# A fp32 decoder layer on one core: DeltaNet's last two units put beside the merge's loads, the MLP's sums put on VectorE, and the RMSNorm ahead of the MLP applied behind its square

## Chip, core and metric

One core of a Trainium2 chip runs the kernel. The metric is the device time of an execution in microseconds. Engines are called by the profile's names: PE is TensorE, DVE is VectorE, ACT is ScalarE, POOL is GpSimd, SP is the engine whose queue issues all DMAs here.

## What is computed

One layer of a decoder with d = 1024, 1024 positions and a hidden width of 4096, all in fp32. Cut to what the change touches:

```python
mix = sigmoid(g_dn) * (o_dn @ W_dn) + sigmoid(g_ns) * (o_ns @ W_nsa)
x   = x + mix @ W_out
h2  = x * rsqrt(mean(x * x, axis=-1) + EPS) * gain
x   = x + square(relu(h2 @ W_up)) @ W_down
```

Ahead of it stand the first RMSNorm, the input projections, a gated DeltaNet (o_dn) and a sparse attention with three branches (o_ns).

## The kernel before

**Number format.** Activations lie with features on the 128 partitions and with positions in the free dimension, in two halves of 512. A fp32 product is made of three matmuls on parts of 32 bits of a shorter mantissa: each operand is split into a high part, copied by ACT (L174), and a low part, which DVE makes by subtracting the high part from the operand (L186, and L277 for weights that `unit` loads); then PE sums high·high, high·low and low·high (`gemm`, L188). So every 128x512 block of weights or activations costs one ACT and one DVE instruction before PE can use it.

**Stages that the change touches**, in order of time in the profile. The sparse attention runs to about 1578 us; its pieces, and the 16 DeltaNet units (half, c) of `dn_part` and `dn_gate` between them, are queued with due times by `at3` and emitted in the order of these times. A DeltaNet unit is 24 matmuls of 128x512 into one bank `g` of the pool `ga`; then `dn_gate` loads the gate's input `gtd` into `th` (one buffer), makes (th + 1) * y on DVE (L1352) and stores the result in the scratch tensor `mxd`. The last two units, c = 6 and 7 of half 1, are due behind everything else. Then comes the merge (`ns_rows`, `ns_merge`; 16 units of 24 matmuls): `ns_rows` loads eight rows of `ond`, the attention's output, through four buffers and splits them; `ns_merge` multiplies them by `w_pn`, gates the result, adds `mxd` (on POOL) and splits the sum. `out_proj` (16 units of 24 matmuls, about 1677 to 1768 us) multiplies by `w_o`, adds x, stores it as `x1d` and sums its squares. `root` turns the sums into 1/sqrt(mean + EPS), with small matmuls, a power on POOL, and a matmul that spreads the result over the partitions; `norm_first` (half 0) and `norm_second` (half 1) multiply x by it and make the sums that the up stage needs.

**MLP.** Both products use Winograd's form of Strassen's scheme, with seven products instead of eight. Up: for each of 16 n, seven products p of 12 matmuls (`up_mm`), whose weights are blocks a11, a12, a21, a22 or sums of them (`weights_of`) and whose other operands are B11, B21, B22 and the sums T1 to T4 (`SIDE`), all made once. `up_out` applies relu and the square on ACT; `up_sums` makes the sums that the down stage wants; all go to the scratch tensor `acd`. Down: for each of two n, seven products of 8 times 12 matmuls (`down_mm`), whose order is in `turns`; the sums of weights and the low parts are made five products ahead (`down_prep`, LEAD). Weights come by `down_load`, activations `bb` from `acd` by `down_side`, x by `x_load`.

**What sets the order.** The program is written as one stream; a scheduler reorders it for each engine by data, buffers and priorities, and each engine then runs its list in that order. SP too: a DMA in its list waits until its data and its buffer are ready, and all later DMAs wait behind it. A pool of buffers that is opened in the place of another waits for all readers of the old one.

Of the kernel before, what the change touches and what calls it, by code (L numbers as in the profile page):

```python
# [20 lines left out]
D = 1024  # L21
# [125 lines left out]
def body(ctx: ExitStack, tc: tile.TileContext, A, out):  # L147
# [74 lines left out]
    for half in range(2):  # L222
# [3 lines left out]
        if half == 0:  # L226
            load_consts(cp, 0)
            cp_raw = [wp.tile([128, 4, 128], F32, name="wr", bufs=3) for _ in range(2)]
            for i in range(2):
                SY.dma_start(cp_raw[i], A["w_cp"][0][:, 4 * i:4 * i + 4])  # L230
# [49 lines left out]
    def unit(src):  # L280
        ks = []
        for i in range(2):
            wr = wp.tile([128, 4, 128], F32, name="wr", bufs=3)
            SY.dma_start(wr, src[:, 4 * i:4 * i + 4])
            ks += parts(wr)
# [181 lines left out]
    def cmp_hidden(u, i):  # L467
# [3 lines left out]
        w1 = wp.tile([128, 4, 128], F32, name="wr", bufs=3)  # L471
# [444 lines left out]
    def fill_nb(u):  # L916
# [3 lines left out]
        def prep():  # L920
            for kp in range(4):
                wr = wp.tile([128, 2, 256], F32, name="wr", bufs=3)
# [415 lines left out]
    def dn_part(half, c, j):  # L1338
        oh, ol = D_["o", half]
        ks = D_["w", half, c]  # L1340
        if j == 0:
            D_["y"] = PL.ga.tile([128, 512], F32, name="g")
# [5 lines left out]
    def dn_gate(half, c):  # L1348
        sl = slice(half * 512, half * 512 + 512)
        th = PL.pr.tile([128, 512], F32, name="th", bufs=1)  # L1350
        SY.dma_start(th, gtd[c, :, sl])
# [4 lines left out]
    for half in range(2):  # L1356
        at3(0.2 + 16 * half, dn_rows, half)
        for c in range(8):
            e = 1.5 + 2 * (8 * half + c)
            if half and c >= 6:  # L1360
                e = 22 + 2 * c
# [15 lines left out]
    shut("po", "pm", "pT", "pS", "ga", "pr")  # L1377
    pool("pf", 4, side="right")
    bank("pq", 4)
# [8 lines left out]
    for half in range(2):  # L1388
        rows_o.append([PL.py.tile([128, 8, 512], F32R, name="o") for _ in range(2)])
        mixes.append([big(True) for _ in range(2)])  # L1390
# [7 lines left out]
    def ns_merge(c, half):  # L1398
# [10 lines left out]
        GP.tensor_tensor(md, md, th, OP.add)  # L1409
        act(mh[:, c], md, AF.Copy, scale=0.5)  # L1410
        V.scalar_tensor_tensor(ml[:, c], md, 0.5, f(mh[:, c]), op0=OP.mult, op1=OP.subtract)

    ns_rows(0)
    for c, half in [(0, 0), (1, 0), (0, 1), (1, 1)] + [(c, half) for c in range(2, 8) for half in range(2)]:
# [7 lines left out]
    x1, sums = [[], []], [None, None]  # L1422
# [3 lines left out]
    def out_proj(half, c):  # L1426
# [9 lines left out]
        SY.dma_start(x1d[c, :, HALF[half]], x)  # L1436
        if c == 0:
            sums[half] = t512(PL.p5, "u", 4)
            act(sums[half], x, AF.Square)
        else:  # L1440
            sq = t512(PL.pw, "tmp", 2)
            act(sq, x, AF.Square)
            (V if half else GP).tensor_tensor(sums[half], sums[half], sq, OP.add)

    def root(half):
        return root_rows(sums[half], PL.pq, "Q", PL.pw, PL.p5.tile([128, 4], F32, name="r4", bufs=1), 2)
# [3 lines left out]
    def sub(o, a, b, eng=None):  # L1450
        (eng or GP).tensor_tensor(o, a, b, OP.subtract)
# [3 lines left out]
    def parts_of(n, src, i, eng=V):  # L1455
        act(R[n][:, i], src)
        sub(R[n][:, 4 + i], src, f(R[n][:, i]), eng)

    def norm_first(r):
        R["raw"] = raw = f(big(False))  # L1460
        R["B11"], R["B21"] = big(True), big(True)
        for k in range(8):
            V.scalar_tensor_tensor(raw[:, k], x1[0][k], cols[:, 8 + k:9 + k], r, op0=OP.mult, op1=OP.mult)
            parts_of("B21" if k >= 4 else "B11", raw[:, k], k % 4)

    def norm_second(r):
        raw = R["raw"]
        R["T2"], R["T3"] = big(True), big(True)
        b12, b22, t = [], [], []

        def head(j):
            b12.append(t512(PL.p5, "b", 4))
            V.scalar_tensor_tensor(b12[j], x1[1][j], cols[:, 8 + j:9 + j], r, op0=OP.mult, op1=OP.mult)
            sub(raw[:, j], b12[j], raw[:, j], V)
            b22.append(t512(PL.p5, "c", 8))
            V.scalar_tensor_tensor(b22[j], x1[1][4 + j], cols[:, 12 + j:13 + j], r, op0=OP.mult, op1=OP.mult)

        def second(j):
            t.append(t512(PL.p5, "c", 8))
            sub(t[j], b22[j], raw[:, j], V)  # L1480
            parts_of("T2", t[j], j)

        head(0)
        for j in range(4):
            if j < 3:
                head(j + 1)
            second(j)
        yield
        for j in range(4):
            sub(b12[j], b22[j], b12[j])  # L1490
            parts_of("T3", b12[j], j)
# [259 lines left out]
```

## Time and profile before

| what | us |
|---|---|
| time, median of 3 executions (lowest, highest) | 2409.52 (2408.16, 2412.6) |
| the profiled execution's own time | 2409.07 |
| its span in the trace | 2407.3 |
| PE busy in the span | 2339.8 |
| DVE busy | 1563.8 |
| ACT busy | 1093.4 |
| POOL busy | 569.0 |

In the timelines a row is: start and duration in us, engine, line of the kernel, operation, output tile <- input tiles, size, number of instructions that are drawn together; in brackets stands how long the engine was idle before it, and which instruction or DMA ended that. SPq rows are DMAs being issued. [...] A matmul's own duration overlaps the next one's, so its pace is read from the starts.

### The profile page before, as it was taken

What the parts mean: (1) busy time and instruction counts of PE and PEld (TensorE: products, weight loads), DVE (VectorE), ACT (ScalarE), POOL (GpSimd) and SP (SyncE); (2) the same over time, 40 slices, a digit from 0 to 9 for tenths busy, and PEclk for the clock granted to TensorE, in tenths of its full rate; (3) what the DMA queues carried; (4) which work ended last, traced back from release to release, by engine and by line L of the source; (5) the groups of instructions that cost most, each with busy time, mean ns of one, the idle gap of its engine ahead of it and who ended that gap; (6) DMA issues with size and microseconds to landing.
All of it is one profiled execution on the core that took longest, in us unless ns stands there. A gap on an engine that the chain in (4) does not pass through costs nothing. (4 is left out here: it accounts for less than half of the span.)

```text
span 2407.3 us, 44378 instructions
## 1 busy us (share of the span) xinstructions
PE 2339.8 (97%) x16673; PEld 1916.8 (80%) x16673; DVE 1563.8 (65%) x3626; ACT 1093.4 (45%) x2258; POOL 569.0 (24%) x473
## 2 busy tenths in 40 slices
PE   7999999999999999999999999999999999989999
PEld 5887878787878887877777777778878888878887
DVE  6766664747484838348877777643397666596785
ACT  4233343434344444227666766532355555534443
POOL 3132321203231423000010111012145444260320
PEclk9999999999999999999999999999999999999999
DMA  5421313131212221237432422164425443566333
GB/s 176 135 65 56 85 43 94 42 91 44 80 50 82 51 77 50 87 116 179 131 115 72 115 89 73 32 225 161 148 83 172 144 149 136 204 232 225 109 126 102
DMA packets 237510, 267.37 MB, mean 111 GB/s; under 512 B 76976, under 2 KB 128496, under 8 KB 237168
## 3 DMA queue, kind: packets, MB, share of 16 engines
q1 hardware_dynamic: 237296, 264.55, 35.2%
q8 instruction: 131, 2.15, 0.4%
q14 instruction: 83, 0.68, 0.1%
HBM read 190.05 MB, written 72.38 MB: 109 GB/s over the span
## 5 line engine op out<-in xcount | busy, mean ns | idle before, releaser
L177 PE MATMUL g<-hh,wh 128*128 128x512 f32 (+1 forms) x816 | 335.4, 411 | 8.2 <-ACT hh L174 7.3
L177 PE MATMUL g<-hl,wh 128*128 128x512 f32 (+1 forms) x816 | 327.4, 401 | 0.1
L177 PE MATMUL g<-hh,wl 128*128 128x512 f32 (+1 forms) x816 | 323.5, 396 | 0.0
L177 PE MATMUL V<-big,wh 128*128 128x512 f32 x768 | 239.4, 392 | 1.6 <-DVE c L1594 1.6
L186 DVE TENSOR_TENSOR wl<-a,wh 128x512 fp32r<-128x512 f32 x192 | 160.6, 838 | 111.0 <-ACT wh L174 110.9
L174 ACT ACTIVATE wh<-wr 128x512 fp32r<-128x512 f32 x210 | 132.1, 630 | 207.1 <-PE g L177 131.4
L174 ACT ACTIVATE wh<-a 128x512 fp32r<-128x512 f32 x192 | 121.1, 631 | 219.6 <-PE V L177 109.5
L1223 DVE CUSTOM_DVE_ANT_0 junk<-S,cst 128x384 f32<-128x384 f32 (+3 forms) x320 | 168.4, 533 | 56.8 <-PE S L177 52.7
L277 DVE TENSOR_TENSOR wl<-wr,wh 128x512 fp32r<-128x512 f32 x178 | 123.6, 698 | 111.9 <-ACT wh L174 108.4
L177 PEld LDWEIGHTS g<-hh,wh 128*128 128x128 f32 (+1 forms) x816 | 153.6, 188 | 36.2 <-ACT hh L174 7.5
L174 ACT ACTIVATE P<-T 128x512 f32<-128x512 f32 x228 | 134.0, 597 | 100.9 <-PE T L177 88.9
L177 PEld LDWEIGHTS g<-hh,wl 128*128 128x128 f32 (+1 forms) x816 | 153.4, 188 | 29.5 <-issue 0.6
L177 PEld LDWEIGHTS g<-hl,wh 128*128 128x128 f32 (+1 forms) x816 | 153.8, 188 | 26.4 <-DVE hl L324 0.8
L177 PEld LDWEIGHTS V<-big,wh 128*128 128x128 f32 x768 | 144.7, 189 | 32.7 <-ACT c L174 1.2
L177 PE MATMUL V<-big,wl 128*128 128x512 f32 x384 | 150.5, 392 | 3.2 <-DVE wl L186 3.2
L177 PE MATMUL g<-wh,hh 128*128 128x256 f32 x512 | 147.4, 288 | 0.0
L177 PE MATMUL g<-wl,hh 128*128 128x256 f32 x512 | 144.8, 283 | 0.0
L177 PE MATMUL g<-wh,hl 128*128 128x256 f32 x512 | 144.8, 283 | 0.0
L1272 POOL TENSOR_TENSOR acc<-acc,bs 128x256 f32<-128x256 f32 x62 | 48.9, 789 | 401.3 <-DVE bs L1270 286.9
L177 PEld LDWEIGHTS o<-vv,P 128*64 128x64 f32 x3648 | 116.0, 138 | 27.1 <-issue 20.4
L177 PE MATMUL o<-vv,P 128*64 128x65 f32 x3648 | 130.1, 225 | 0.0
L177 PE MATMUL S<-ks,qc 96*128 96x384 f32 (+3 forms) x320 | 127.1, 409 | 1.6 <-DVE mx L1223 1.4
(371 smaller groups left out, 5709.1 us busy)
## 6 DMA issues: line engine op xcount, KB each, us to landing
bb<-acd SPq DMA_DIRECT2D x112, 256.0 KB, 2.8
wr<-in_w_dn_dram SPq DMA_DIRECT2D x64, 256.0 KB, 2.9
a<-in_w_u_dram SPq DMA_DIRECT2D x64, 256.0 KB, 3.4
acd<-c SPq DMA_DIRECT2D x64, 256.0 KB, 3.0
a<-in_w_d_dram SPq DMA_DIRECT2D x64, 256.0 KB, 4.9
wr<-in_w_nb_dram SPq DMA_DIRECT2D x32, 256.0 KB, 2.7
wr<-in_w_gt_dram SPq DMA_DIRECT2D x32, 256.0 KB, 2.7
gtd<-fx SPq DMA_DIRECT2D x32, 256.0 KB, 2.2
```

What stands on the lines that cost most here:

```text
L174: return SC.activation(o, i, fn, **kw)
L177: return PE.matmul(o, l, r, start=start, stop=stop, skip_group_check=True)
L186: V.tensor_tensor(lo, src, f(hi), OP.subtract)
L277: V.tensor_tensor(wl, wr, f(wh), OP.subtract)
L1223: V.tensor_tensor_reduce(junk[:, :w], ps[:, :w], mask[:, a:b], 1.0, 3e38, OP.add, OP.min, o)
L1272: adds.tensor_tensor(acc, acc, b, OP.add)
```

## The change

1. The DeltaNet units c = 6 and 7 of half 1 leave the schedule of the sparse stage. Only their weights are loaded there. They are written behind the first `ns_rows`; their gates' inputs are loaded into two buffers of the merge's pool; c = 7 sums in a bank of its own (pool `pT`); the pools of the sparse stage are closed behind them.
2. Raw weights of `unit` are staged in the pool `cq` (3 buffers), which is closed before the merge; from then on in two buffers `a22` of the merge's pool `pw`. Before, three buffers in a pool that stays open served all stages.
3. All sums of tiles in SBUF run on DVE; POOL had them: the merge's 16 sums, 7 sums of squares, and most sums of the MLP.
4. Since relu(r·z)² = r²·relu(z)², the MLP starts from x times gain, which ACT makes in `out_proj`; r² = 1/(mean + EPS) comes from one matmul with a matrix of ones, a multiply and add, and a DVE reciprocal of 128x512 for each half; `up_out` multiplies by it (four products for each n). The sums for half 1 are made within `out_proj`.
5. Down, n = 0: product order 4, 2, 1, 5, 6, 3, 7 instead of 1, 2, 6, 5, 7, 3, 4; the blocks a22 are loaded first, a11 later; x tiles are loaded in another order.

```diff
-            cp_raw = [wp.tile([128, 4, 128], F32, name="wr", bufs=3) for _ in range(2)]
+            cp_raw = [PL.cq.tile([128, 4, 128], F32, name="wr", bufs=3) for _ in range(2)]
...
     def unit(src):
...
-            wr = wp.tile([128, 4, 128], F32, name="wr", bufs=3)
+            if hasattr(PL, "pw"):
+                wr = PL.pw.tile([128, 512], F32, name="a22", bufs=2).rearrange("p (a b) -> p a b", a=4)
+            else:
+                wr = PL.cq.tile([128, 4, 128], F32, name="wr", bufs=3)
...
-            D_["y"] = PL.ga.tile([128, 512], F32, name="g")
+            D_["y"] = PL.pT.tile([128, 512], F32, name="T") if half and c == 7 else PL.ga.tile([128, 512], F32, name="g")
...
             if half and c >= 6:
-                e = 22 + 2 * c
+                at3(e - 0.5, dn_weights, half, c)
+                continue
...
-        GP.tensor_tensor(md, md, th, OP.add)
+        V.tensor_tensor(md, md, th, OP.add)
...
+    ths = []
+    for c in (6, 7):
+        ths.append(t512(PL.pw, "a12"))
+        SY.dma_start(ths[-1], gtd[c, :, HALF[1]])
     ns_rows(0)
+    for c in (6, 7):
+        for j in range(4):
+            dn_part(1, c, j)
+        dn_gate(1, c, ths[c - 6])
+    shut("po", "pm", "pT", "pS", "ga", "pr")
+    pool("pf", 4, side="right")
+    bank("pq", 4)
...
         SY.dma_start(x1d[c, :, HALF[half]], x)
+        if half == 0:
+            y = raw[:, c]
+        else:
+            y = t512(PL.p5, *(("b", 4) if c < 4 else ("c", 8)))
+            (b12 if c < 4 else b22).append(y)
+        act(y, x, AF.Copy, scale=cols[:, 8 + c:9 + c])
...
-            (V if half else GP).tensor_tensor(sums[half], sums[half], sq, OP.add)
+            V.tensor_tensor(sums[half], sums[half], sq, OP.add)
...
     def root(half):
-        return root_rows(sums[half], PL.pq, "Q", PL.pw, PL.p5.tile([128, 4], F32, name="r4", bufs=1), 2)
+        p = t512(PL.pq, "Q")
+        mm(p, K("ones"), sums[half], True, True)
+        rr[half] = r = sums[half]
+        V.tensor_scalar(r, p, 1.0 / D, EPS, op0=OP.mult, op1=OP.add)
+        V.reciprocal(r, r)
...
-    def sub(o, a, b, eng=None):
-        (eng or GP).tensor_tensor(o, a, b, OP.subtract)
+    def sub(o, a, b):
+        V.tensor_tensor(o, a, b, OP.subtract)
...
+    def norm_second(j):
+        sub(raw[:, j], b12[j], raw[:, j])
+        t2s.append(t512(PL.p5, "u", 4))
+        sub(t2s[j], b22[j], raw[:, j])
+        sub(b12[j], b22[j], b12[j])
+        sub(raw[:, 4 + j], raw[:, 4 + j], t2s[j])
...
-            GP.tensor_tensor(a21, a21, a22, OP.add)
+            V.tensor_tensor(a21, a21, a22, OP.add)
...
         act(x, x, AF.Square)
+        r = rr[p in (0, 3)]
+        V.tensor_tensor(x, x, r, OP.mult)
...
-    turns = [(1, 2, 6, 5, 7, 3, 4), (2, 1, 5, 6, 3, 7, 4)]
+    turns = [(4, 2, 1, 5, 6, 3, 7), (2, 1, 5, 6, 3, 7, 4)]
...
-            DW[n, i, b] = t = t512(PL.pg if d == 0 else PL.ph, b, J)
+            DW[n, i, b] = t = t512(PL.pg if m else PL.ph, b, J)
...
-        if n and p == 1:
+        if p == 1:
             sub(w["a11"], w["a11"], w["a21"])
-        e = q - J - 5
-        if 0 <= e < J:
-            sub(DW[0, e, "a11"], DW[0, e, "a11"], DW[0, e, "a21"])
...
         if (half, c) == (1, CB):
-            norm_first(root(0))
+            root(0)
+            norm_first()
+        if half and c >= 4:
+            norm_second(c - 4)
+    norm_parts("T2")
...
-        if q == 2:
-            second = norm_second(root(1))
-        if q in (2, 7, 8):
-            next(second)
+        if q in (2, 4, 6, 8):
+            norm_parts(("T3", "T4", "T1", "B22")[q // 2 - 1])
+        if q == 3:
+            root(1)
```

How the change stands in the engines' lists, at three places. **SP where the merge begins**, before (a_18952 to a_18980 are the first eight rows of `ond`, a_18996 and a_18997 the inputs of the first merge unit's gate):

```order
L1404 DMA a_18996<-gtd 128x512
L1353 DMA mxd<-th 128x512
L1395 DMA a_18968<-ond 128x512
L1395 DMA a_18972<-ond 128x512
L1395 DMA a_18976<-ond 128x512
L1351 DMA th<-gtd 128x512
L1395 DMA a_18980<-ond 128x512
L1405 DMA a_18997<-mxd 128x512
L1395 DMA a_19029<-ond 128x512
L1395 DMA a_19033<-ond 128x512
L1353 DMA mxd<-th 128x512
```

and with the change (a_18878 and a_18880 are the two gates' inputs and then their results, a_18882 to a_18910 the eight rows, a_18984 and a_18990 the raw weights of the first merge unit):

```order
L1396 DMA a_18894<-ond 128x512
L1357 DMA mxd<-a_18878 128x512
L1396 DMA a_18898<-ond 128x512
L1396 DMA a_18902<-ond 128x512
L1396 DMA a_18906<-ond 128x512
L1396 DMA a_18910<-ond 128x512
L1357 DMA mxd<-a_18880 128x512
L287 DMA a_18984<-in_w_pn_dram 128x512
L287 DMA a_18990<-in_w_pn_dram 128x512
L1405 DMA a_18996<-gtd 128x512
L1406 DMA a_18997<-mxd 128x512
```

The loads of the two gates' inputs now stand ahead of the rows, and the loads of `w_pn`, which stood among the last items of the sparse stage, stand behind the store of the last gate.

**DVE at the first root**, before (tile r is 128x4; wl<-wr are low parts of `w_o`):

```order
L1435 TENSOR_TENSOR c<-c,V 128x512
L241 TENSOR_SCALAR r_20137<-Q 128x4
L277 TENSOR_TENSOR wl<-wr,wh 128x512
L1443 TENSOR_TENSOR u<-u,tmp 128x512
L252 TENSOR_TENSOR tmp<-cst_114,r_20137 128x512
L277 TENSOR_TENSOR wl<-wr,wh 128x512
L1463 SCALAR_TENSOR_TENSOR big<-a_19659,cols,Q 128x512
L1463 SCALAR_TENSOR_TENSOR big<-a_19733,cols,Q 128x512
L1463 SCALAR_TENSOR_TENSOR big<-a_19809,cols,Q 128x512
```

and with the change (s_19690 and s_19723 are the sums of squares of half 0 and half 1, c<-c,V the addition of x in `out_proj`; L1478 is `sub`, a_20227 and a_20233 are raw `w_o` of the unit (1, 5)):

```order
L1451 TENSOR_TENSOR c<-c,V 128x512
L1478 TENSOR_TENSOR big<-big 128x512
L1472 TENSOR_SCALAR s_19690<-Q 128x512
L1478 TENSOR_TENSOR big<-big 128x512
L1465 TENSOR_TENSOR s_19723<-s_19723,tmp 128x512
L1473 RECIPROCAL s_19690<-s_19690 128x512
L1451 TENSOR_TENSOR c<-c,V 128x512
L277 TENSOR_TENSOR wl<-a_20227,wh 128x512
L277 TENSOR_TENSOR wl<-a_20233,wh 128x512
L1478 TENSOR_TENSOR u<-c,big 128x512
L1465 TENSOR_TENSOR s_19723<-s_19723,tmp 128x512
```

The reciprocal stands between the addition of one unit and the next, with the low parts of a later unit's weights behind it.

**DVE in the first products of the down stage that use sums of weights**, before (al is the low part of an activation, tmp the difference of two weight blocks, a_22958 and a_22962 blocks a11):

```order
L186 TENSOR_TENSOR wl<-tmp,wh 128x512
L186 TENSOR_TENSOR al<-bb,ah 128x512
L1451 TENSOR_TENSOR tmp<-a_23253,a_22958 128x512
L186 TENSOR_TENSOR al<-bb,ah 128x512
L186 TENSOR_TENSOR wl<-tmp,wh 128x512
L1451 TENSOR_TENSOR tmp<-a_23279,a_22962 128x512
L186 TENSOR_TENSOR al<-bb,ah 128x512
L186 TENSOR_TENSOR wl<-tmp,wh 128x512
L1451 TENSOR_TENSOR tmp<-a_23309,a_22966 128x512
L186 TENSOR_TENSOR al<-bb,ah 128x512
L186 TENSOR_TENSOR wl<-tmp,wh 128x512
```

and with the change (a_22995 and a_22999 are blocks a22, a_23247 and a_23273 blocks a11, a_23249 and a_23275 blocks a21, a_23121 a block a12; L1515 is the sum for p = 5):

```order
L1478 TENSOR_TENSOR a_23247<-a_23247,a_23249 128x512
L186 TENSOR_TENSOR al<-bb,ah 128x512
L1515 TENSOR_TENSOR a_23249<-a_23249,a_22995 128x512
L1478 TENSOR_TENSOR tmp<-a_22995,a_23247 128x512
L186 TENSOR_TENSOR wl<-a_23273,wh 128x512
L186 TENSOR_TENSOR al<-bb,ah 128x512
L1478 TENSOR_TENSOR a_23273<-a_23273,a_23275 128x512
L1478 TENSOR_TENSOR a_23121<-a_23121,tmp 128x512
L186 TENSOR_TENSOR wl<-a_23301,wh 128x512
L1515 TENSOR_TENSOR a_23275<-a_23275,a_22999 128x512
L186 TENSOR_TENSOR al<-bb,ah 128x512
```

Between two low parts of activations there stood one difference and one low part of it; now four or five rows, among them the sums that POOL had.

## Rows read from the trace of the kernel before

**Rows 1.** The page, part 1, TensorE: busy us (share), instructions.
```profile
PE 2339.8 (97%) x16673; PEld 1916.8 (80%) x16673; DVE 1563.8 (65%) x3626; ACT 1093.4 (45%) x2258; POOL 569.0 (24%) x473
```

**Rows 2.** Five stretches: PE, PEld, DVE, ACT, POOL busy (instructions), clock, DMA, GB/s.
```profile
1768.00:1790.00 22.00, 19.84 (x88) 15.48 (x87) 20.15 (x24) 10.28 (x18) 18.01 (x13) 1.00 0.07 25
1790.00:1810.00 20.00, 16.17 (x57) 12.46 (x58) 20.00 (x26) 13.24 (x24) 9.40 (x6) 0.83 0.19 66
1810.00:2075.00 265.00, 264.16 (x1166) 218.45 (x1165) 173.86 (x201) 151.16 (x255) 113.59 (x71) 1.00 0.43 145
2075.00:2130.00 55.00, 54.22 (x240) 44.57 (x239) 40.34 (x50) 27.70 (x47) 20.63 (x13) 1.00 0.92 330
2130.00:2156.00 26.00, 18.83 (x69) 14.15 (x68) 23.54 (x20) 4.91 (x9) 24.92 (x16) 0.90 0.37 122
```

**Rows 3.** Timeline where the merge begins: start, us, instruction [idle before <-releaser].
```profile
1579.36 0.50 PE L177 MATMUL g<-oh,wh 128*128 128x512 f32 x1 [0.78 <-DVE th L1352]
...
1584.47 0.32 SPq L1351 DMA_DIRECT2D th<-gtd  x1
...
1589.17 0.69 DVE L1352 SCALAR_TENSOR_TENSOR th<-th,g 128x512 f32<-128x512 f32 x1 [1.11 <-DMA th<-gtd]
...
1589.96 1.19 PE L177 MATMUL V<-o,wh 128*128 128x512 f32 x2 [4.86 <-issue]
...
1594.60 0.40 PE L177 MATMUL V<-o,wl 128*128 128x512 f32 x1
```

**Rows 4.** Timeline of SP: an early load of the merge’s weights.
```profile
1489.23 0.33 SPq L284 DMA_DIRECT2D wr<-in_w_pn_dram  x1
```

**Rows 5.** The page, part 6: DMA issues, KB each, median us to landing.
```profile
wr<-in_w_dn_dram SPq DMA_DIRECT2D x64, 256.0 KB, 2.9
```

**Rows 6.** Timeline of TensorE where the MLP begins.
```profile
1773.49 0.95 PE L177 MATMUL Q<-cst,u 128*128 128x1 f32 x8
...
1778.46 1.10 PE L177 MATMUL Q<-tmp,cst 128*128 128x512 f32 x2 [1.58 <-DVE tmp L252]
...
1796.84 0.79 PE L177 MATMUL V<-big,wl 128*128 128x512 f32 x1 [3.16 <-DVE wl L186]
...
1802.55 0.40 PE L177 MATMUL Q<-big,wl 128*128 128x512 f32 x1
```

**Rows 7.** Timeline of TensorE where the down stage begins.
```profile
2140.22 0.59 PE L177 MATMUL Q<-al,wh 128*128 128x512 f32 x1 [2.23 <-DVE al L186]
...
2143.97 0.39 PE L177 MATMUL Q<-al,wh 128*128 128x512 f32 x1
...
2153.95 0.66 PE L177 MATMUL Q<-ah,wl 128*128 128x512 f32 x1 [1.18 <-DVE wl L186]
...
2157.39 0.47 PE L177 MATMUL Q<-al,wh 128*128 128x512 f32 x1
```

**Rows 8.** Timeline of VectorE: beside GpSimd (first), and without it.
```profile
2133.16 1.76 DVE L186 TENSOR_TENSOR al<-bb,ah 128x512 fp32r<-128x512 f32 x1
...
2199.38 0.69 DVE L186 TENSOR_TENSOR wl<-a,wh 128x512 fp32r<-128x512 f32 x1 [1.43 <-ACT wh L174]
2199.99 0.69 DVE L186 TENSOR_TENSOR al<-bb,ah 128x512 fp32r<-128x512 f32 x1
```

**Rows 9.** VectorE, groups by form: count | busy us, mean ns | idle before.
```profile
L186 DVE TENSOR_TENSOR al<-bb,ah 128x512 fp32r<-128x512 f32 x112 | 98.3, 879 | 0.9 <-ACT ah L174 0.8
...
L1266 DVE RECIPROCAL coef<-o 128x4 f32<-128x4 f32 x64 | 11.5, 180 | 51.3 <-PE o L177 51.0
...
L1594 DVE TENSOR_TENSOR c<-c,V 128x512 f32<-128x512 f32 x16 | 10.8, 676 | 3.3 <-PE V L177 3.3
...
L419 DVE RECIPROCAL s<-s 128x64 f32<-128x64 f32 x1 | 0.5, 546 | 0.0
```

**Rows 10.** Two stretches of 50 us, columns as in rows 2.
```profile
1800.00:1850.00 50.00, 49.15 (x210) 39.92 (x209) 41.71 (x52) 32.19 (x56) 25.84 (x15) 0.97 0.50 169
2200.00:2250.00 50.00, 50.00 (x223) 41.39 (x222) 31.15 (x51) 20.78 (x36) 0.00 (x0) 1.00 0.53 175
```


## Prediction made before the run

> **What bounds the kernel now.** I read the page's busy shares first, then PE's waits, then busy times by stretch, then single timelines at the places that the change touches. PE is busy for 97% of the span [rows 1], so only three things can move the end: PE's work, PE's waits, and the clock. In a stretch where PE never waits, 223 matmuls take 50 us [rows 10], 0.224 us each, whatever DVE and POOL do meanwhile. The up stage is such a stretch: from 1810 to 2075 us PE is busy for 264.16 of 265 us [rows 2]. PE's time is lost at three places, and the change touches all three.
>
> First, where the merge begins. PE waits 0.78 us between the two DeltaNet units and 4.86 us ahead of the first merge matmul, which starts right after the gate at 1589.17; that gate had waited for `th`, whose load was issued at 1584.47, when the other unit's store had freed its only buffer [rows 3]. Second, where the MLP begins (1768 to 1810): PE is idle for 2.16 and then 3.83 us, DVE is busy all the time, and the mean clock falls to 0.83 [rows 2]. Third, where the down stage begins (2130 to 2156): PE is idle for 7.17 us, DVE is busy for 23.54 and POOL for 24.92 of 26 us, at 20 and 16 instructions [rows 2]. After a wait PE runs at half its rate for a while: the 11 matmuls from 1589.96 to 1594.60 take 4.64 us instead of 2.46 [rows 3]. So a wait costs more than its length.
>
> Why DVE is late there is in its own rows. Beside a POOL sum a DVE subtraction takes 1.76 us; where POOL rests two start 0.61 us apart, though each is shown with 0.69 [rows 8]. Additions that read PSUM keep 0.68 on the mean [rows 9].
>
> **The change part by part.** The sum is made against the profiled execution, 2409.07 us; the median lies 0.45 above it.
>
> *Sums from POOL to DVE.* DVE gets some 150 instructions that POOL had and loses the slow ones: 0.61 each by the pace without POOL, 31.15 us for 51 instructions [rows 10]. In the up stage DVE's list has 23 instructions for one n of seven products: 14 that it had, 3 sums of weights, 2 sums of outputs and 4 multiplications by r². That is 14.0 us at 0.61, against 84 matmuls by 0.224, 18.8 us. PE covers it; the cover is gone above 18.8/23 = 0.82 us an instruction. In the stretch from 1800 to 1850, beside a POOL that is half busy, DVE needs 0.80 (41.71 for 52) [rows 10]; that is the dear end. I take 0.61, since POOL has nothing left in these stages. ACT's 16 new copies lie in `out_proj`, off PE's path. Up stage and merge units: 0.
>
> *The norm.* Lost before: 2.16 + 3.83 idle, 2.8 at half rate (13 matmuls from 1796.84 to 1802.55 take 5.71 instead of 2.91), and 1.6 for two rows of eight matmuls of one column, the second from 1773.49 (0.95 as shown, 0.8 of it not under the next matmul) [rows 2, 6]: 10.4 us. The wait for the spread root, 1.58 at 1778.46 [rows 6], is in the first number. All this goes, since no product waits for r any more; only the multiplications behind the square do. New are two DVE reciprocals of 128x512. Rows give 180 ns for 4 columns and 546 for 64 [rows 9], 6.1 ns a column, so 3.3 us each as an estimate. The first stands in DVE's list ahead of the low parts of `w_o` of the unit (1, 5): with the five instructions beside it 6.3 us, against the unit's 24 matmuls, 5.4 us. I replayed DVE's list from there with 0.61 an instruction, 3.3 a reciprocal and PE's matmuls at 0.224: PE waits about 1.7 us at (1, 5), 0.3 at (1, 1), 1.6 at the first product with p = 6, behind the second reciprocal, and 0.2 elsewhere: 3.8 us, a guess within 2. With 0.69 an instruction, the shown duration taken as the pace, the same replay gives 11.2. I take 0.61, because it is what consecutive starts show. Term: 3.8 - 10.4 = -6.6, ends -10.4 (no wait left) and +0.8.
>
> [...] The two rows [rows 9] speak for 3.3; no run here shows one of 512.
>
> *The down stage's start.* Lost before: 7.17 idle and 3.4 at half rate (9 matmuls from 2140.22 to 2143.97 and 8 from 2153.95 to 2157.39 take 3.75 and 3.44 us instead of 2.0 and 1.8) [rows 2, 7]: 10.6 us. The low parts `al` that PE waits for stand behind sums made by POOL and DVE at 1.7 us each; on DVE alone a product has at most five instructions, 3.1 us, and most have two or three, against 12 matmuls, 2.7 us, with five products of lead. The new order of n = 0 puts the products with sums later. I leave 0.3. What could be late next is a load: from 2075 to 2130 the DMA engines are busy for 0.92 at 330 GB/s [rows 2], and a22 and a12 are now needed first. Before, PE lost only 0.78 us in that stretch [rows 2], with the same bytes to move. Term: -10.3, ends 0 and -10.6.
>
> *The merge's start.* The wait of 0.78 goes: unit 7 has its own bank. `th` is loaded early: the wait of the last gate for its load goes too. But the first merge unit's weights, of which the first load was issued at 1489.23 [rows 4], now wait for the pool and stand on SP behind four rows and the store of that gate; behind SP's wait stand also the inputs of the first merge gates, which are not needed for 5 us. PE's list still has the first merge matmul behind the gate, as before. Unit 7 ends at 1584.3; the gate stands on DVE behind the low parts of four rows, and I put it at 1586.8; store and load issue follow at 1587.4, the load lands 2.9 later [rows 5], and ACT's copy and PE follow at about 1591.4 instead of 1589.96. Half rate behind it stays. Term: +1.4; ends -1 (the gate right behind unit 7) and +4 (rows and weights landing in each other's way).
>
> Sum: +1.4 - 6.6 - 10.3 = -15.5 us, that is 2393.6.
>
> **Rivals.** (A) DVE's pace in the norm is 0.69, not 0.61: the waits there stay at 11.2, the other terms hold: 2393.6 + 7.4 = 2401.0. For it speaks that 0.69 is what each row shows; against it the starts [rows 8]. Chance 0.13.
>
> (B) The down stage's waits only change their name, from DVE to a DMA, because blocks a22, a12 and the activations come together while the DMA engines are full [rows 2]: 2393.6 + 10.3 = 2403.9. Against it: PE kept 54.22 of 55 us in that stretch. Chance 0.10. With A as well it is 2411.3; chance 0.04.
>
> (C) The wait ahead of the merge really goes, because rows, gate and weights all land before unit 7 ends: first merge matmul at 1584.3, and the 2.2 us of half rate gone too: 1.4 becomes -7.8, so 2384.4. Against it speaks SP's order. Chance 0.06.
>
> (D) Slower: DVE becomes the bound in the MLP. It decides at 0.82 us an instruction; the low parts `al` have 0.88 on the mean now [rows 9]. At 0.87 one n takes 20.0 us instead of 18.8, 19 us over 16 n; the norm's waits by the same replay come to about 22 instead of 3.8; and the 36 instructions in the eight products with p = 6 of the down stage take 31.3 instead of 21.6 us, 9.7 more: 2393.6 + 19 + 18 + 9.7 = 2440. Against it: where POOL rests DVE keeps 0.61 [rows 10]. Chance 0.07. [...]
>
> (E) Part 1 does not do what it says: c = 7 has its own bank, yet the merge still waits for its gate. That is in the forecast.
>
> **How the numbers follow.** Forecast 0.60, A 0.13, B 0.10, C 0.06, D 0.07, A and B 0.04. A measurement of this kernel can tell about 0.2%, 4.8 us, from no change: faster is below 2404.7, slower above 2414.3. Forecast, A, C and 0.07 of B give faster, 0.86; the rest of B and the double case give no difference, 0.07; D gives slower, 0.07. The range goes from 2385 (forecast with the merge's -1 and the norm's -10.4, and part of C) to 2404 (A and most of B); left out are D, the double case, and edges of B and C, under 0.2 together.
>
> **What would show it.** Right: DVE's subtractions at 0.69 throughout, none at 1.76; idle plus half rate between 1744 and 1810 near 4 us, behind reciprocals of 3.3; PE without a wait for the first 300 us of the down stage; the first merge matmul 5 to 7 us behind unit 7, released by `w_pn`. Wrong: PE waiting for DVE all through the up stage (D); waits for DMA in the first down products (B); reciprocals far over 3.3 us; a first merge matmul right behind unit 7 (C).

## The result and the profile after

The changed kernel takes 2393.99 us (median of 4 executions, 2391.62 to 2395.04), the kernel before 2409.17 (median of 4); the ratio is 0.9933, with a 95% interval from 0.9916 to 0.995. So it is faster by 15 us, 0.7%. The forecast was 2393.6. The profiled execution took 2395.04 us, its span is 2393.3; before it was 2409.07 and 2407.3.

To see where the 14.0 us between the two spans went, I cut the time behind the sparse stage into pieces between matmuls that both kernels have: the last matmul on `acc` (the sparse stage's end), and the first and last matmul of the stages behind it. Every number is a difference of two starts in the trace.

| piece | before | after | difference |
|---|---|---|---|
| span's start to the last matmul on `acc` | 1575.24 | 1577.82 | +2.58 |
| from there to the first matmul of out_proj (last units, merge) | 103.94 | 107.81 | +3.87 |
| out_proj | 88.87 | 89.16 | +0.29 |
| up stage | 318.54 | 309.82 | -8.72 |
| first to last matmul of the down stage | 316.47 | 304.41 | -12.06 |
| from there to the end | 4.24 | 4.24 | 0.00 |

The page's first part (compare [rows 1]) shows PE with 5.6 us less, mostly the matmuls that ran at half rate in [rows 6, 7] and no longer do, and POOL at 304.7 us instead of 569.0:

```profile
PE 2334.2 (98%) x16657; PEld 1913.4 (80%) x16657; DVE 1601.6 (67%) x3837; ACT 1101.4 (46%) x2274; POOL 304.7 (13%) x308
```

The stretches that answer to [rows 2], with the same columns (the stages lie a few us differently; the clock is the mean that PE was granted, as a share of full speed, and the share behind it is the DMA engines' busy time):

```profile
1764.00:1810.00 46.00, 44.02 (x189) 34.76 (x188) 44.72 (x71) 29.03 (x54) 0.00 (x0) 1.00 0.27 92
1810.00:2073.00 263.00, 263.00 (x1162) 217.78 (x1161) 206.14 (x324) 149.49 (x253) 0.00 (x0) 1.00 0.40 145
2073.00:2130.00 57.00, 56.22 (x248) 46.17 (x248) 44.63 (x71) 29.57 (x50) 0.00 (x0) 1.00 0.95 338
2130.00:2160.00 30.00, 30.00 (x134) 24.86 (x133) 25.16 (x42) 13.22 (x23) 0.00 (x0) 1.00 0.81 269
```

POOL has no instruction left in any of them. Where the MLP begins PE is idle for 2 us of 46 instead of 6 of 42, and where the down stage begins for none of 30 instead of 7.2 of 26. In the up stage DVE is busy for 78% of the time instead of 66%, and PE does not wait for it. What PE still waits for in `out_proj` and the up stage, from the timeline of PE:

```profile
1758.77 0.50 PE L177 MATMUL V<-big,wl 128*128 128x512 f32 x1 [0.93 <-DVE wl L277]
...
1782.57 0.50 PE L177 MATMUL Q<-big,wl 128*128 128x512 f32 x1 [0.86 <-DVE wl L186]
...
1799.24 0.74 PE L177 MATMUL Q<-big,wh 128*128 128x512 f32 x2 [0.48 <-ACT wh L174]
1800.38 0.50 PE L177 MATMUL Q<-big,wl 128*128 128x512 f32 x1 [0.40 <-DVE wl L186]
...
1803.63 0.73 PE L177 MATMUL Q<-big,wh 128*128 128x512 f32 x2 [0.24 <-ACT b L174]
...
2081.71 0.50 PE L177 MATMUL V<-big,wh 128*128 128x512 f32 x1 [0.79 <-DVE c L1597]
```

The first wait stands where the replay had put one, at the unit (1, 5) behind the first reciprocal, though at 0.9 instead of 1.7 us. The second is at (1, 1), 0.86 instead of 0.3. The next three are those at the first p = 6 and just behind it, behind the second reciprocal, 1.1 together instead of 1.6. The last, at the end of the up stage, stood there before the change too. VectorE by form, behind the sparse stage (columns as in [rows 9]), shows the new price of an instruction and of a reciprocal:

```profile
L186 DVE TENSOR_TENSOR wl<-a,wh 128x512 fp32r<-128x512 f32 x192 | 131.9, 689 | 73.8 <-ACT wh L174 73.6
L186 DVE TENSOR_TENSOR al<-bb,ah 128x512 fp32r<-128x512 f32 x112 | 76.9, 687 | 2.3 <-ACT ah L174 2.0
...
L1473 DVE RECIPROCAL s<-s 128x512 f32<-128x512 f32 x2 | 6.7, 3348 | 0.0
```

Subtractions that took 0.88 us on the mean are at 0.69, and 512 columns of reciprocal take 3.35 us, against 3.3 worked out from 4 and 64 columns.

The place that got worse is the start of the merge (compare [rows 3]). The timeline there:

```profile
1578.26 0.33 SPq L1418 DMA_DIRECT2D a<-gtd  x1
...
1579.63 1.92 SPq L1396 DMA_DIRECT2D a<-ond  x4
...
1585.70 2.57 ACT L174 ACTIVATE o<-a 128x512 fp32r<-128x512 f32 x4 [7.08 <-DMA a<-ond]
...
1587.09 2.25 SPq L1396 DMA_DIRECT2D a<-ond  x4
1588.91 0.68 DVE L1356 SCALAR_TENSOR_TENSOR a<-a,T 128x512 f32<-128x512 f32 x1
...
1589.99 0.94 SPq L287 DMA_DIRECT2D a<-in_w_pn_dram  x2
...
1594.97 1.31 ACT L174 ACTIVATE wh<-a 128x512 fp32r<-128x512 f32 x2 [1.73 <-DMA a<-in_w_pn_dram]
...
1595.65 1.22 PE L177 MATMUL V<-o,wh 128*128 128x512 f32 x2 [9.02 <-ACT wh L174]
...
1607.52 0.73 PE L177 MATMUL V<-o,wh 128*128 128x512 f32 x2 [0.65 <-ACT wh L174]
```

PE waits 9.02 us instead of 0.78 + 4.86. The first of the four rows that are issued from 1579.63 on reaches ACT at 1585.70, 6 us after its issue; the last gate runs at 1588.91; the weights are issued at 1589.99, right behind its store, and ACT can copy them at 1594.97, 5 us later. The second unit's weights are late as well: PE waits for them for 0.65 us more at 1607.52.

### The profile page after: what moved, and what is told of

Same layout as the page of the kernel before. It is cut to its first block, busy times and chain, and to the rows that moved or that the text cites. A ratio compares the mean times of both kernels' runs of the same rounds, so it can differ in the third digit from the quotient of the medians.

```text
span 2393.3 us, 44220 instructions
## 1 busy us (share of the span) xinstructions
PE 2334.2 (98%) x16657; PEld 1913.4 (80%) x16657; DVE 1601.6 (67%) x3837; ACT 1101.4 (46%) x2274; POOL 304.7 (13%) x308
## 4 chain that ended last, share of the span: by engine, by line
PE 49%; DVE 2%; DMA 1%; ACT 1%; issue 0%; POOL 0%; SPq 0%; ACTq 0%; POOLq 0%; DVEq 0%
PE V L177 19%; PE Q L177 12%; PE T L177 5%; PE o L177 5%; PE g L177 3%; PE S L177 2%; PE m L177 1%; DMA a<-ond 1%; PE m L1280 0%; DVE big L1478 0%; DVE junk L1226 0%; PE m L1193 0%; DMA ra<-odd 0%; POOL acc L1275 0%; DMA a<-in_w_o_dram 0%
## 5 line engine op out<-in xcount | busy, mean ns | idle before, releaser
L174 ACT ACTIVATE wh<-a 128x512 fp32r<-128x512 f32 x234 | 146.7, 629 | 251.0 <-PE V L177 155.4
L186 DVE TENSOR_TENSOR wl<-a,wh 128x512 fp32r<-128x512 f32 x192 | 131.9, 689 | 73.8 <-ACT wh L174 73.6
L174 ACT ACTIVATE wh<-wr 128x512 fp32r<-128x512 f32 x168 | 105.5, 629 | 157.4 <-PE g L177 128.1
L277 DVE TENSOR_TENSOR wl<-wr,wh 128x512 fp32r<-128x512 f32 x136 | 94.7, 701 | 90.5 <-ACT wh L174 89.5
L676 DVE SCALAR_TENSOR_TENSOR acc<-xp,cols,acc 128x512 f32<-128x512 f32 x144 | 117.0, 812 | 6.2 <-ACT acc L174 4.8
```

Of the source, the lines that this page charges most:

```text
L174: return SC.activation(o, i, fn, **kw)
L186: V.tensor_tensor(lo, src, f(hi), OP.subtract)
L277: V.tensor_tensor(wl, wr, f(wh), OP.subtract)
L676: V.scalar_tensor_tensor(a2, xp[:, i:i + 512], cols[:, c0 + i:c0 + i + 1], a2, op0=OP.mult, op1=OP.add)
```

## The experiments

All are compared by the same pieces. In this section "merge" is the piece from the last matmul on `acc` to the first one of out_proj.

**The kernel before, with only the sums moved to VectorE** (dve_sums). Of the change's parts it has part 3 alone.

```diff
-        GP.tensor_tensor(md, md, th, OP.add)
+        V.tensor_tensor(md, md, th, OP.add)
...
-            (V if half else GP).tensor_tensor(sums[half], sums[half], sq, OP.add)
+            V.tensor_tensor(sums[half], sums[half], sq, OP.add)
...
-        (eng or GP).tensor_tensor(o, a, b, OP.subtract)
+        (eng or V).tensor_tensor(o, a, b, OP.subtract)
```

> The kernel before, with nothing changed but the engine of the sums: all tile sums of the merge, out_proj and the MLP on VectorE. Theory (sharing of SBUF between VectorE and GpSimd slows VectorE, which makes TensorE wait): VectorE's subtractions take 0.69 us everywhere behind the merge, the down stage (first down matmul to last) shrinks from 316.5 us to under 306, and from the first up product to the first down matmul from 318.5 to 312 to 315, because the chain over the root stays; in all 13 to 17 us under the kernel before, 2392 to 2396. Rival (the root's chain and the order of the down products cost the time): within 3 us of the kernel before, 2406 to 2412, and the waits of the down stage stay.

Measured: 2399.11 us, ratio 0.9949 (0.9932 to 0.9966) to the kernel before, 2410.67 on that chip. Down stage 304.41 us, the whole gain of the change there. Up stage 318.87: no gain at all. Subtractions and waits of PE:

```profile
L186 DVE TENSOR_TENSOR al<-bb,ah 128x512 fp32r<-128x512 f32 x112 | 76.9, 687 | 1.5 <-ACT ah L174 1.4
```

```profile
1800.28 0.74 PE L177 MATMUL Q<-big,wh 128*128 128x512 f32 x2 [2.31 <-ACT b L174]
...
1805.79 0.50 PE L177 MATMUL V<-big,wh 128*128 128x512 f32 x1 [0.50 <-ACT big L174]
...
1813.20 0.73 PE L177 MATMUL Q<-big,wh 128*128 128x512 f32 x2 [1.77 <-ACT wh L174]
1814.67 0.50 PE L177 MATMUL Q<-big,wl 128*128 128x512 f32 x1 [0.73 <-DVE wl L186]
```

The time lies between the two expectations. So the theory holds for the down stage and falls for the up stage. There DVE is fast now (0.69 us for each of the 112 `al`), but the products still cannot start before the root, and the sums that POOL had now stand in DVE's list behind it; PE waits for `b`, `big` and `wh` a little later than before, 7.0 us in all instead of 7.6. That what the two engines share is SBUF was the author's guess and is not isolated by a run; the traces show which forms slowed. `al`, with both operands in SBUF, took 0.88 us on the mean in the kernel before and takes 0.69 here; the 16 additions c<-c,V of L1590, with one operand in PSUM, took 0.68 in the kernel before, where 15 of them ran wholly beside a POOL instruction, and take 0.68 in the changed kernel, where POOL rests.

**The changed kernel, with the sums back on GpSimd** (pool_sums), where the kernel before had them. It has all parts but part 3; calls of `sub` that ran on VectorE before the change stay there, by a last argument `V`.

```diff
-        V.tensor_tensor(md, md, th, OP.add)
+        GP.tensor_tensor(md, md, th, OP.add)
...
-    def sub(o, a, b):
-        V.tensor_tensor(o, a, b, OP.subtract)
+    def sub(o, a, b, eng=None):
+        (eng or GP).tensor_tensor(o, a, b, OP.subtract)
```

> The changed kernel, with the sums back on GpSimd where the kernel before had them. Theory (sharing): subtractions beside GpSimd at 1.7 us again; waits come back where the sums stand close: 3 to 8 us from the first up product to the first down matmul and 3 to 10 us in the down stage; 2400 to 2410. Rival (the norm's new form and the new order give the gain): within 3 us of the changed kernel, 2391 to 2397.

Measured: 2415.78 us, ratio 1.0024 (1.0012 to 1.0037): slower than the kernel before by 0.2%, and outside both expectations. The pieces are those of the profiled execution, which took 2411.33 us, 4.5 less than the median of 10 (2411.08 to 2425.27). Out_proj takes 93.16 us and the up stage 323.26, together 9.0 us more than before the change; the down stage takes 307.27, 9.2 less. PE's waits where the MLP begins, and two forms of VectorE:

```profile
1786.30 2.08 PE L177 MATMUL Q<-s,cst 128*128 128x512 f32 x2 [3.32 <-DVE s L1465]
...
1805.46 0.50 PE L177 MATMUL Q<-big,wl 128*128 128x512 f32 x1 [2.13 <-DVE wl L186]
...
1815.15 1.22 PE L177 MATMUL Q<-big,wh 128*128 128x512 f32 x2 [4.39 <-ACT b L174]
```

```profile
L186 DVE TENSOR_TENSOR al<-bb,ah 128x512 fp32r<-128x512 f32 x112 | 98.9, 885 | 2.3 <-ACT ah L174 2.1
...
L1478 DVE TENSOR_TENSOR c<-c,u 128x512 f32<-128x512 f32 x16 | 27.5, 1716 | 0.0
```

The two runs and the two kernels make a square:

| | out_proj + up: root ahead of the MLP | root behind its square | down: old order | new order |
|---|---|---|---|---|
| sums on POOL | 407.41 (before) | 416.42 (pool_sums) | 316.47 (before) | 307.27 (pool_sums) |
| sums on VectorE | 407.74 (dve_sums) | 398.98 (after) | 304.41 (dve_sums) | 304.41 (after) |

Where the MLP begins neither part gains alone, and the new norm alone loses 9 us: PE waits 14.6 us in these two pieces of pool_sums instead of 7.6. The new norm puts the sums of half 1, the reciprocals and 64 multiplications on a DVE that POOL slows (0.885 us for `al` instead of 0.687); which of them cost how much was not tried. Together they gain 8.4. In the down stage either part would do most of it alone: the new order takes 9.2 of the 12.1 us and the sums all of it, so that with the sums moved the new order is worth nothing.

**The weights of the first merge unit loaded first** (wpn_first).

```diff
+    first = []
+    for i in range(2):
+        first.append(PL.pw.tile([128, 512], F32, name="a22", bufs=2).rearrange("p (a b) -> p a b", a=4))
+        SY.dma_start(first[-1], A["w_pn"][0][:, 4 * i:4 * i + 4])
     ns_rows(0)
```

> The changed kernel, with the two loads of the first merge unit's weights issued ahead of the eight rows instead of behind the last gate's store. In the changed kernel the first merge matmul starts 17.8 us after the last matmul on acc of the sparse stage, and 6.1 us after the end of the last gate. Theory (TensorE waits for that load, which lands 5 us after a late issue): the first merge matmul starts within 1 us of the last gate's end, 12 to 14 us after the last matmul on acc; 4 to 6 us less in all, 2388 to 2390. Rival 1 (the loads only change places: the rows land later and TensorE waits for them): 15 to 17 us after, 1 to 3 us less. Rival 2 (the wait is for the gate's bank): no change.

Measured: 2395.74 us, ratio 0.9936 (0.9921 to 0.9951); merge 107.64 us against 107.81. The first merge matmul does come 11.4 us after the last one on `acc` instead of 17.8, but then PE waits inside the merge:

```profile
1590.80 0.70 PE L177 MATMUL V<-o,wh 128*128 128x512 f32 x2 [2.58 <-ACT o L174]
...
1597.35 0.50 PE L177 MATMUL V<-o,wh 128*128 128x512 f32 x1 [1.51 <-ACT o L174]
...
1603.81 1.22 PE L177 MATMUL V<-o,wh 128*128 128x512 f32 x2 [4.12 <-ACT wh L174]
```

It waits for ACT's copy of a row, again for a row, and then 4.12 us for the second unit's weights. Rival 1 holds, further than it was priced: the gain is gone to the last 0.2 us, less than this piece scatters. It is not one late load: rows, gate inputs and weights all have to come in the 20 us after the merge's pools open, and from 1578 to 1606 the DMA engines move 238 GB/s on the mean, with medians from issue to landing of 5.1 us for rows and 4.0 for weights, against the 2.9 of [rows 5]. The mean rate alone does not tell the kernels apart: the kernel before moved 278 GB/s from 1578 to 1606. The weights of the first two units were not among what had to land there: it had fetched this MB in four loads from 1489.23 [rows 4] to 1531.39, each in 2.5 to 3.4 us.

**The DeltaNet units back in the sparse schedule** (no_dn): part 1 undone, the rest as changed.

```diff
             if half and c >= 6:
-                at3(e - 0.5, dn_weights, half, c)
-                continue
+                e = 22 + 2 * c
...
+    shut("po", "pm", "pT", "pS", "ga", "pr")
     ns_rows(0)
-    for c in (6, 7):
-        for j in range(4):
-            dn_part(1, c, j)
-        dn_gate(1, c, ths[c - 6])
-    shut("po", "pm", "pT", "pS", "ga", "pr")
```

> The changed kernel, with the last two DeltaNet units back in the sparse schedule (one bank, one buffer for the gate's input); the staging of weights stays as changed. Theory (moving the units gains nothing by itself, and puts the loads of the merge's weights behind the last gate): the first merge matmul 14.5 to 16 us after the last matmul on acc, as before the change (14.7), instead of 17.8; 2 to 3 us less than the changed kernel, 2391 to 2392. Rival (the move gains its 0.8 us wait and more, and the staging pays for it): 18 us after or later, 2394 to 2397.

Measured: 2391.94 us, ratio 0.9924 (0.991 to 0.9939). The first merge matmul comes 13.26 us after the last one on `acc`, and the merge takes 105.21, 2.6 less than in the changed kernel. PE's waits:

```profile
1590.65 1.19 PE L177 MATMUL V<-o,wh 128*128 128x512 f32 x2 [3.38 <-issue]
...
1602.44 0.49 PE L177 MATMUL V<-o,wl 128*128 128x512 f32 x1 [1.56 <-DVE wl L277]
```

The wait of 1.56 us for the second unit's weights is what the late staging still costs: dve_sums, which has the old staging and the old schedule, needs 103.45. So of the 4.4 us between 103.45 and 107.81 the move of the units costs 2.6 and the staging 1.8. That split is good to about 1 us: runs below repeat the merge with the same lists of instructions on every engine, and it takes 108.76 (no_recip) against 107.81, and 104.07 (best) against 105.21.

**Staging and units as before the change, with two buffers instead of three** (no_dn_wr2). The pool p5 of the changed kernel is larger; a version with three buffers beside it was not run.

```diff
-            if hasattr(PL, "pw"):
-                wr = PL.pw.tile([128, 512], F32, name="a22", bufs=2).rearrange("p (a b) -> p a b", a=4)
-            else:
-                wr = PL.cq.tile([128, 4, 128], F32, name="wr", bufs=3)
+            wr = wp.tile([128, 4, 128], F32, name="wr", bufs=2)
```

> The changed kernel with the DeltaNet units back in the sparse schedule and the raw weights staged as before the change, in a pool that stays open, but in two buffers instead of three. Theory (both parts of the change at the merge cost: the move 2.6 us, the late weights 1.8): from the last matmul on acc to the first out_proj matmul 103 to 104.5 us, as in the kernel before (103.94) and with its sums on VectorE (103.45), against 107.81 in the changed kernel and 105.21 with the units alone put back; the rest as in the changed kernel. Rival (two buffers make earlier stages wait for weights, or the merge's weights come late again): 105 us or more, or over 1 us more TensorE idle ahead of 1570 us.

Measured: 2399.97 us, ratio 0.9963 (0.9949 to 0.9977). The merge takes 103.09, as the theory said; but the last matmul on `acc` comes at 1586.79 instead of 1577.82, so the rival holds too. In the first 130 us, here and in the changed kernel:

```profile
40.00:60.00 20.00, 16.97 (x89) 13.09 (x88) 12.17 (x38) 3.51 (x10) 4.38 (x7) 1.00 0.71 206
60.00:80.00 20.00, 15.52 (x73) 12.61 (x71) 12.31 (x20) 4.25 (x9) 1.75 (x3) 0.83 0.41 116
80.00:130.00 50.00, 45.64 (x255) 37.46 (x255) 29.44 (x50) 11.06 (x22) 2.62 (x4) 0.97 0.37 105
```

```profile
40.00:60.00 20.00, 18.65 (x100) 14.70 (x98) 12.60 (x39) 3.62 (x10) 3.99 (x7) 1.00 0.68 187
60.00:80.00 20.00, 17.90 (x87) 14.95 (x88) 12.56 (x20) 5.26 (x11) 1.75 (x3) 0.83 0.55 173
80.00:130.00 50.00, 49.04 (x285) 40.37 (x283) 35.55 (x60) 13.81 (x26) 9.20 (x9) 1.00 0.34 102
```

PE is busy for 78.1 of these 90 us against 85.6: with two buffers the loads of the first stages come too late. For loads of `in_cw_dram` PE waits 4.6 us in three waits, 2.0 at most, where the changed kernel waits 1.1 us in two, 0.8 at most. From about 43 us on PE's list stands in another order, too. The gain at the merge is paid twice over ahead of it.

**The reciprocals left out** (no_recip).

```diff
         V.tensor_scalar(r, p, 1.0 / D, EPS, op0=OP.mult, op1=OP.add)
-        V.reciprocal(r, r)
```

> The changed kernel with the two reciprocals left out (the MLP is scaled by the mean square instead of its inverse). It measures what the two instructions of 3.35 us cost on the path. Theory (they stand ahead of low parts that TensorE waits for): from the first out_proj matmul to the first down matmul 2 to 4 us less than the 398.98 of the changed kernel, and the wait of 0.93 at the unit (1, 5) gone. Rival (VectorE's whole queue is full there, and the waits only move): less than 1 us less.

Measured: 2392.3 us in one execution; out_proj and up together 394.58 us against 398.98, so 4.4 less for two instructions of 3.35, a little more than expected. The waits of the first reciprocal and of p = 6 are gone; in the up stage only the one of 0.78 at its end is left. Of the 4.4 us 2.9 are waits; most of the rest are starts next to a wait, which stand further apart. VectorE's list is full in this stretch (44.72 of 46 us busy from 1764 to 1810 in the changed kernel), and of the 6.7 us taken out of it 4.4 reach PE.

**The second root later** (late_root).

```diff
-        if q == 3:
+        if q == 10:
             root(1)
```

> The changed kernel with the second root called at the eleventh product of the up stage instead of the fourth. Theory (the second reciprocal stands in VectorE's busiest stretch, ahead of the low parts for p = 6; later VectorE has 4 us to spare for each n): from the first up matmul to the first down matmul 1.5 to 2.5 us less than 309.82. Rival (the low parts behind it are late anyway, or it delays the products for which TensorE has no lead later): within 0.7 us of 309.82.

Measured: 2393.71 us, ratio 0.9933 (0.9918 to 0.9947), up stage 308.01 us, 1.8 less. Alone this is too small for the measurement of the whole; the piece shows it. PE's waits in the up stage are down to

```profile
1782.57 0.50 PE L177 MATMUL Q<-big,wl 128*128 128x512 f32 x1 [1.00 <-DVE wl L186]
```

and the one of 0.78 at the end.

**The last two edits together** (both):

> The two last edits together: units and staging as before the change, second root late. If both theories hold: 4 us less than the changed kernel at the merge and 2 less in the up stage, 2387 to 2390, against 2391 to 2394 if only one holds, and 2394 or more if none does.

Measured: 2398.42 us, ratio 0.9955 (0.9942 to 0.9969). Merge 102.90, up stage 307.97: both savings are there, but the last matmul on `acc` comes at 1588.98, as in no_dn_wr2; the two buffers take more than both give.

**Units back, second root late, staging as changed** (best):

> The changed kernel with the two DeltaNet units back in the sparse schedule and the second root at the eleventh product; staging as changed. If both savings add up: from the last matmul on acc to the first out_proj matmul 105 to 105.5 us instead of 107.81, from the first up matmul to the first down matmul 308 instead of 309.82; together 4 us under the changed kernel measured beside it, about 2389 to 2391. Rival (they don't add, or the time ahead of the merge scatters more than they give): within 2 us of the changed kernel.

Measured: 2389.87 us, ratio 0.9905 (0.9886 to 0.9924), against 2394.11 for the changed kernel on the same chip. Merge 104.07, 1 us under the expectation and no_dn; up stage 308.12, down stage 304.42. It is faster than both kernels, 21 us under the kernel before.

**The changed kernel again** (after_again):

> The changed kernel once more, on the chip of the last run: 2392 to 2396 us, and stage by stage within 0.3 us of its first profile behind the last matmul on acc of the sparse stage (107.8, 89.2, 309.8, 304.4). Theory (the time ahead of that matmul scatters with the granted clock of the first 80 us): that matmul starts anywhere from 1573 to 1580 us. Rival (the staging pool sets it): at 1577.8 within 0.5.

Measured: 2394.11 us, ratio 0.9933 (0.9917 to 0.9949). Merge 107.53, out_proj 89.16, up 309.70, down 304.42: the pieces repeat within 0.3 us. The last matmul on `acc` starts at 1577.28, which tells the two accounts of the scatter hardly apart; the other runs do. pool_sums, with the changed staging, has it at 1573.24, and dve_sums, with the old staging, at 1577.83. Up to 1490 us the two run the same list of DMAs, and at a store at 1469.64 and 1474.26 they are already 4.6 us apart; behind it dve_sums loads four blocks of the merge's weights that pool_sums loads later. Busy times of the stretches from 20 to 40 and from 60 to 80 us, in pool_sums and then in the changed kernel's first profile:

```profile
20.00:40.00 20.00, 16.20 (x67) 10.78 (x66) 16.33 (x19) 8.46 (x16) 10.52 (x8) 0.91 0.05 15
60.00:80.00 20.00, 17.71 (x98) 14.74 (x98) 15.54 (x26) 6.30 (x13) 1.74 (x3) 1.00 0.58 174
```

```profile
20.00:40.00 20.00, 15.82 (x59) 9.84 (x58) 16.26 (x19) 7.84 (x15) 9.87 (x7) 0.83 0.07 21
60.00:80.00 20.00, 17.90 (x87) 14.95 (x88) 12.56 (x20) 5.26 (x11) 1.75 (x3) 0.83 0.55 173
```

The mean granted clock differs, 0.91 and 1.00 against 0.83 and 0.83, and the arrival at the next stage by 3 us. One stretch shows that it is the clock. It starts with the same wait of 0.87 us, holds the same 82 matmuls, and has no wait above 0.12 us; in pool_sums and then in the changed kernel:

```profile
63.80:79.40 15.60, 15.46 (x82) 12.81 (x82) 11.59 (x21) 5.53 (x12) 1.22 (x2) 1.00 0.47 140
```

```profile
64.20:82.60 18.40, 18.28 (x82) 14.85 (x82) 11.68 (x22) 5.44 (x11) 1.23 (x2) 0.83 0.40 119
```

## Why the prediction was right

**The time.** The forecast was -15.5 us; the medians differ by 15.2, the two spans by 14.0. The sum is better than its terms: two pieces came out later than forecast, by 2.5 and 2.6 us, and two earlier, by 1.8 each. That they nearly cancel is luck; the 2.6 of the sparse stage were in no term.

**The norm** (-6.6 forecast, -8.4 measured over out_proj and up). The mechanism held: no product waits for r, and PE's waits after are 0.93 + 2.77 = 3.7 us, against 3.8 from the replay at 0.61 us an instruction. The total agrees better than its parts: the waits behind the reciprocals came out shorter, and 0.79 at the end of the up stage was not in the replay. What was mis-sized is the time beside these waits. With 0.2265 us for each of the 1728 matmuls (the pace of the down stage), the two pieces hold 16.0 us of loss before, 7.6 of it waits, and 7.6 after, 3.7 of it waits; the sum had 10.4 and 3.8. Before, a wait of 0.84 at 1816 lay outside the stretch that was summed. Nor does half rate follow every wait: behind the 3.16 us at 1796.84 13 matmuls stand 0.43 us apart and more, behind each wait of 0.93 and less after the change only one stands 0.34 behind the last, and the granted clock there is 1.00, where it was 0.53 from 1796 to 1803 before. The two reciprocals cost 4.4 us on the path, as no_recip shows, more than the waits alone. The square adds what the prediction didn't say: the two parts work only together. A reciprocal of 512 columns takes 3.35 us; the estimate from the rows of 4 and 64 columns, 3.3, held.

**The down stage** (-10.3 forecast, -12.1 measured). Right, and no wait is left: 1344 matmuls take 304.41 us, 0.2265 each. Of the 1.8 us more, 0.3 had been left for waits that didn't come, 0.2 are one more wait, at 2294, and 1.2 lie in the starts next to the waits, which cost 4.6 us over the pace instead of the 3.4 that were summed. The step that gave the new order a share was wrong: dve_sums has the old order and the same 304.41.

**The merge** (+1.4 forecast, +3.9 measured, inside its ends of -1 and +4). The gate was sized right: 1586.8 forecast, 1588.91 measured, of which 2.6 are the late arrival of everything. The step that failed is "the load lands 2.9 later": it took 5.0, behind four rows and a store that were issued in the 3 us before it. That explains 1.7 of the 2.5 us; most of the rest is the wait for the second unit's weights. That the transfers beside it made the load slow is likely but not isolated by a run. And wpn_first shows that the step was too narrow: with this load early, the rows and the next weights take its place.

**What was not in it.** The sparse stage's end came 2.6 us later in the profile. That is scatter of the kernel's first 80 us, not the change. At the first matmul on `acc` the changed kernel is already 3.6 us late, with the same lists of instructions on every engine up to there, and dve_sums, whose sparse stage is that of the kernel before, arrives at 1577.83. Over the kernels with three staging buffers the last matmul on `acc` starts anywhere from 1573.24 to 1579.40.

**The rivals.** A, an instruction at 0.69 with 11.2 us of waits: they came to 3.7. B, waits for DMA in the first down products: none. C, the merge's wait gone: it grew, from 4.86 to 9.02. D, VectorE as the bound: 263.00 of 263 us of PE in the up stage. E held: the merge still starts behind the last gate.

## What to carry to other kernels

A sum on GpSimd beside VectorE was not free work here: 163 sums moved onto an engine that was already the late one made it earlier, because its own subtractions fell from 1.76 us beside a POOL sum [rows 8] to 0.69, of which 0.61 counts. Two parts of a change can be worth nothing or less alone and 8 us together, or each can bring most of the same 12 us; run the square of both before crediting either. Work that is moved to the seam between two stages competes with the loads that the seam must make (in wpn_first the first weights came earlier, and PE then waited 2.58, 1.51 and 4.12 us for rows and the next weights): ask not only where one load stands, but how many must land in the same 20 us, and leave in place what was fetched ahead.

## What was not expected of the hardware

The granted clock in the first 80 us differs from one profile to the next with the same instructions there (from 60 to 80 us 1.00 before, 0.83 after), and what follows starts up to 3.6 us apart, seen at the first matmul tp<-cst,acc (111.1 us before, 114.7 after). The difference in the whole span to the sparse stage's end reaches 6.2 us; differences of kernels under 0.2% are safer to read from pieces between matmuls than from whole times. What makes the clock differ there was not tried.
